# Cross-covariance attention: V moved up by one unit, and a tail written out by hand after the last gram

## The chip, the cores and the metric

The kernel runs on one core of a Trainium2 chip. The core has five engines with an instruction stream each: TensorE (PE; its weight loads are listed apart as PEld), VectorE (DVE), ScalarE (ACT), GpSimd (POOL) and SyncE (SP), which here issues every transfer between the chip's main memory (HBM) and the on-chip memory. The engines run side by side and wait for each other through semaphores; each works through its own instructions in the order in which the program wrote them. Matrix products land in PSUM, from where ACT or DVE copies them out. The metric is the device time of one execution in microseconds (us); the median of several runs is compared.

## The reference

Q, K and V have 8 batches, 12 heads, 512 positions and 64 features, all float32. Attention runs over the features, not over the positions:

```python
Q_norm = Q / (np.linalg.norm(Q, axis=-2, keepdims=True) + 1e-10)
K_norm = K / (np.linalg.norm(K, axis=-2, keepdims=True) + 1e-10)
attn = np.einsum('bhnd,bhne->bhde', Q_norm, K_norm)
attn = np.exp(attn - np.max(attn, axis=-1, keepdims=True))
attn = attn / (np.sum(attn, axis=-1, keepdims=True) + 1e-10)
return np.einsum('bhnd,bhde->bhne', V, attn)
```

So each head needs a 64x64 matrix of logits, which is complete only when all 512 positions of Q and K are in, a softmax over its rows, and then a product of V with that small matrix.

## The kernel before

The 96 heads are taken four at a time: a unit is four heads, and there are U = 24 units. For each unit Q, K and V are one transfer of 512 KB each, and so is the output. In all, SP issues 96 transfers.

What is done for a unit u, by the names of the functions:

- `load_qk`, `load_v`, `store`: the transfers, all on SP.
- `cast_q`, `cast_k` (DVE): Q and K to bf16, side by side in one tile `qkb`. `cast_v` (ACT): V to bf16, tile `vb`.
- `grams` (PE, 64 products): the product of [Q K] with itself, accumulated over the positions in the PSUM tile `gbuf`. One result holds the sums of squares on its diagonal and the raw logits off it. There is one `gbuf`, so the next unit's grams wait until this one's are read.
- `norms` (DVE, then POOL): the diagonal into `nsq` by four reductions, then its power -0.5 on POOL into `rq`. `keep_kq` (ACT): the logits, still unscaled, into `kq`.
- `scale_k` (DVE): `kq` times the norms of K gives `kqs`. `logits` (PE): transposes it into PSUM. `scale_q` (DVE): times the norms of Q gives `sl`. `exps` (ACT): the exponential `ex`.
- `normalise` (DVE, three instructions): row sums, their reciprocals, and the normalised bf16 matrix into the upper half of one of three buffers `ab`. `doubled` (PE, then ACT): a copy of it into the lower half, so that two heads can be multiplied at once. The logits and this duplicate share one PSUM tile.
- `vtrans` (PE, eight transposes, then an ACT copy): V with the features on the partitions, tile `vt`.
- `outs` (PE, 16 products; ACT, two copies): the output of the unit through two PSUM buffers `po` into `so`, which `store` sends.

The order is written by hand. One loop, over steps s, issues for several units at a time, each function at its own distance behind the grams of unit s:

```python
LOAD_AHEAD = 3
V_AHEAD = LOAD_AHEAD - 3
STORE_LAG = 6
```

Q and K are loaded three units ahead, V for the unit of the same step. Softmax work (`scale_k`, `logits`, `scale_q`, `exps`) is for unit s-1; `normalise`, `doubled`, `cast_v` and `vtrans` for unit s-2; `outs` for unit s-3; the store for unit s-6. A call outside 0 to U-1 is skipped by `on`, so the loop runs three steps past the last gram, to s = U+2, and its last three steps hold only what is left over. Because each engine keeps the program's order, a function's place in the step is also its place in its engine's queue.

Of the kernel before, what the change touches and what calls it, by code (L numbers as in the profile page):

```python
# [24 lines left out]
def kernel(  # L25
# [7 lines left out]
    nc = tc.nc  # L33
    B, H, N, _ = Q.shape
    assert N == NV * R and Q.shape[3] == D
    U = B * H // HU
# [17 lines left out]
    ps_o = ctx.enter_context(tc.tile_pool(name="ps_o", bufs=2, space=bass.MemoryType.PSUM))  # L54

    LOAD_AHEAD = 3
    V_AHEAD = LOAD_AHEAD - 3
    STORE_LAG = 6

    qf, kf, vf, vb, qkb, nsq, rq, kqs, sl, ex, vt, so, kq = ({} for _ in range(13))  # L60

    def load_qk(u):
        qf[u] = qp.tile([128, R, D], F32, name="qf")
        kf[u] = qp.tile([128, R, D], F32, name="kf")
        nc.sync.dma_start(out=qf[u].rearrange("p t d -> p (t d)"), in_=Qf[u])  # L65
        nc.sync.dma_start(out=kf[u].rearrange("p t d -> p (t d)"), in_=Kf[u])  # L66

    def load_v(u):
        vf[u] = vp.tile([128, SV, TP * 2 * D], F32, name="vf")
        nc.sync.dma_start(out=vf[u], in_=Vf[u])  # L70

    def store(u):
        nc.sync.dma_start(out=Of[u], in_=so[u].rearrange("p s t d -> p s (t d)"))
# [5 lines left out]
    def cast_k(u):  # L79
        nc.vector.tensor_copy(qkb[u][:, :, D:], kf[u])  # L80

    def cast_v(u):
        w = vb[u] = vbp.tile([128, SV, TP, 2 * D], BF16, name="vb")
        nc.scalar.copy(w.rearrange("p s t d -> p s (t d)"), vf[u])  # L84

    def grams(u):

# [22 lines left out]
    def scale_k(u):  # L110

        kk = kqs[u] = small.tile([128, HU, D], F32, name="kqs")
        nc.vector.tensor_tensor(  # L113
            out=kk[D:], in0=kq[u][D:], in1=rq[u][D:, :, None].to_broadcast([D, HU, D]), op=ALU.mult,
        )

    def logits(u):
        for h in range(HU):
            nc.tensor.transpose(lg[:, h, :], kqs[u][D:, h, :], ident[D:, D:])  # L119

    def scale_q(u):
        s = sl[u] = small.tile([D, HU, D], F32, name="sl")
        nc.vector.tensor_tensor(out=s, in0=lg, in1=rq[u][0:D, :, None].to_broadcast([D, HU, D]), op=ALU.mult)  # L123

    def exps(u):
        e = ex[u] = small.tile([D, HU, D], F32, name="ex")
        nc.scalar.activation(e, sl[u], AF.Exp)  # L127

    def normalise(u):
        s = small.tile([D, HU], F32, name="esum")  # L130
        nc.vector.reduce_sum(out=s, in_=ex[u], axis=AX.X)  # L131
        ri = small.tile([D, HU], F32, name="rinv")
        nc.vector.reciprocal(ri, s)
        a = abuf[u % len(abuf)]
        nc.vector.tensor_tensor(out=a[0:D, :, 0, :], in0=ex[u], in1=ri[:, :, None].to_broadcast([D, HU, D]), op=ALU.mult)  # L135

    def vtrans(u):

        ps = ps_v.tile([128, SV, TP, 128], BF16, name="vps")
        for g in range(SV):  # L140
            for t in range(TP):
                nc.tensor.transpose(ps[:, g, t, :], vb[u][:, g, t, :], identb)  # L142
        w = vt[u] = vtp.tile([128, SV, TP, 128], BF16, name="vt")
        nc.scalar.copy(w, ps)  # L144

    def doubled(u):

        a = abuf[u % len(abuf)]
        nc.tensor.matmul(dup[D:], identb[0:D, 0:D], a[0:D, :, 0, :], tile_position=(0, D))  # L149
        nc.scalar.copy(a[D:, :, 1, :], dup[D:])  # L150

    def outs(u):
        s = so[u] = sop.tile([128, SV, TP, 2 * D], F32, name="so")
        a = abuf[u % len(abuf)]
        for g in range(SV):
            po = ps_o.tile([128, TP, 2 * D], F32, name="po")
            for t in range(TP):
                for x in range(2):
                    rows = slice(MV * x, MV * (x + 1))
                    nc.tensor.matmul(  # L160
                        po[rows, t, :], vt[u][:, g, t, rows],
                        a[:, 2 * g + x].rearrange("p a d -> p (a d)"), tile_position=(0, MV * x),
                    )
            nc.scalar.copy(s[:, g], po)  # L164
# [6 lines left out]

    for u in range(LOAD_AHEAD):
        load_qk(u)

    ident = const.tile([128, 128], F32, name="ident")
    make_identity(nc, ident)
# [10 lines left out]
    def on(f, u):  # L187
        if 0 <= u < U:
            f(u)

    on(cast_q, 0)
    on(cast_k, 0)
    for s in range(U + 3):
        on(load_qk, s + LOAD_AHEAD)
        on(load_v, s + V_AHEAD)
        on(store, s - STORE_LAG)
        on(cast_v, s - 2)
        on(cast_q, s + 1)
        on(normalise, s - 2)
        on(scale_k, s - 1)  # L200
        on(grams, s)
        on(norms, s)
        on(cast_k, s + 1)
        on(doubled, s - 2)
        on(keep_kq, s)
        on(outs, s - 3)
        on(logits, s - 1)
        on(scale_q, s - 1)
        on(exps, s - 1)
        on(vtrans, s - 2)  # L210
    for u in range(U + 3 - STORE_LAG, U):
        store(u)


# [28 lines left out]
```

## Time and profile before

Four runs took 136.02 to 136.83 us, with a median of 136.13. The profile is of one more execution, which took 136.24 us; its span from the first to the last instruction is 134.5 us, with 1.74 us around it.

| engine | busy us | share of the span | instructions |
|---|---|---|---|
| PE (matmul) | 88.3 | 66% | 2232 |
| PEld (weight load) | 68.4 | 51% | 2232 |
| DVE | 94.6 | 70% | 360 |
| ACT | 97.9 | 73% | 169 |
| POOL | 36.1 | 27% | 35 |
| transfers of the kernel | - | 95.7% of 16 DMA engines | 96 |

No compute engine is busy for more than three quarters of the span. The transfers read 37.75 MB and write 12.58 MB, with a mean of 374 GB/s over the span.

How to read what follows: a row of the timeline has the start in us from the beginning of the span, the duration in us, the engine, the line of the kernel, the operation, what it writes <- what it reads, the number of merged instructions, and in brackets how long the engine had stood idle and for whom. SPq is SP issuing a transfer. The chain of waits starts from the last instruction and goes back, at each step, to what released it. The rows of slices cut the span into 40 equal pieces; each digit is a share in tenths, with 9 for 90% or more. The granted clock is the share of its full speed at which TensorE was allowed to run; its mean here is 0.827.

### The profile page before, as it was taken

To read this page: it belongs to the slowest core of one execution; us is meant where nothing else is said; L and a number is where in the kernel's file an instruction comes from. 1 tells how busy PE (TensorE), PEld (TensorE's weight loads), DVE (VectorE), ACT (ScalarE), POOL (GpSimd) and SP (SyncE) were. 2 spreads that over 40 slices of the span, in tenths; PEclk is the share of its full clock that TensorE was granted. 3 is DMA by queue.
4 is the path that set the end of the run, shared out by engine and by line. 5 is a ranking of instruction groups with operands and counts; after the bars stand their busy time and mean duration, and the time that the engine had idled before them with its cause. 6 is when DMAs were issued, how large, how long until landed. Compare 5 with 4: busy or idle time off the path is not lost.

```text
span 134.5 us, 5399 instructions
## 1 busy us (share of the span) xinstructions
PE 88.3 (66%) x2232; PEld 68.4 (51%) x2232; DVE 94.6 (70%) x360; ACT 97.9 (73%) x169; POOL 36.1 (27%) x35
## 2 busy tenths in 40 slices
PE   0146669766674986566645974979984669957630
PEld 0135457555453865454433862756862556745420
DVE  0477957988987898887956887967887967654100
ACT  3011268898889898988966796697796697999950
POOL 7023233244413541343123033033033032120000
PEclk9999999999999599999995599555589965586555
DMA  4999999999999999999999999999999999997444
GB/s 146 388 417 403 403 405 401 398 396 403 397 413 403 414 401 411 408 405 401 410 413 404 413 403 414 411 412 408 409 408 410 402 409 409 399 376 277 162 156 156
DMA packets 19991, 50.67 MB, mean 377 GB/s; under 512 B 1536, under 2 KB 1536, under 8 KB 19968
## 3 DMA queue, kind: packets, MB, share of 16 engines
q1 hardware_dynamic: 19968, 50.34, 95.7%
q8 instruction: 17, 0.28, 0.8%
q14 instruction: 6, 0.05, 0.1%
HBM read 37.75 MB, written 12.58 MB: 374 GB/s over the span
## 4 chain that ended last, share of the span: by engine, by line
DMA 47%; ACT 17%; PE 14%; DVE 9%; issue 6%; SPq 3%; ACTq 0%; DVEq 0%
DMA vf<-in_V_dram 47%; PE gram L91 5%; ACT so L164 4%; ACT vb L84 4%; ACT vt L144 3%; DVE scr L103 3%; PE vps L142 3%; PE lgdup L119 3%; PE po L160 3%; ACT ab L150 2%; ACT ex L127 2%; ACT kq L96 1%; SPq L65 1%; SPq L66 1%; DVE kqs L113 1%
## 5 line engine op out<-in xcount | busy, mean ns | idle before, releaser
L108 POOL TENSOR_TENSOR rq<-nsq,mhalf 128x4 f32<-128x4 f32 x24 | 33.7, 1402 | 82.7 <-DVE nsq L103 82.7
L91 PE MATMUL gram<-qkb 32*128 32x128 bf16 x1536 | 35.0, 254 | 13.1 <-DVE qkb L80 8.9
L91 PEld LDWEIGHTS <-qkb 32*128 32x128 bf16 x1536 | 29.2, 113 | 17.2 <-DVE qkb L80 9.4
L84 ACT CAST vb<-vf 128x1024 bf16<-128x1024 f32 x24 | 25.1, 1047 | 13.0 <-DMA vf<-in_V_dram 13.0
L164 ACT COPY so<-po 128x512 f32<-128x512 f32 x48 | 25.8, 589 | 1.5 <-PE po L160 1.0
L160 PEld LDWEIGHTS <-vt 128*64 128x64 bf16 x384 | 15.3, 136 | 19.5 <-ACT vt L144 14.1
L103 DVE CUSTOM_DVE_ANT_0 scr<-gram,ident 128x128 f32<-128x128 f32 x96 | 22.2, 287 | 3.6 <-PE gram L91 3.1
L144 ACT COPY vt<-vps 128x1024 bf16<-128x1024 bf16 x24 | 24.0, 1001 | 0.6
L160 PE MATMUL po<-ab,vt 128*64 128x128 bf16 x384 | 20.1, 263 | 2.3 <-ACT vt L144 1.2
L77 DVE CAST qkb<-qf 128x1024 bf16<-128x1024 f32 x24 | 16.4, 682 | 7.0 <-DMA qf<-in_Q_dram 6.9
L119 PE MATMUL lgdup<-ident,kqs 64*64 64x64 f32 x96 | 12.1, 260 | 12.7 <-ACT ab L150 12.7
L123 DVE TENSOR_TENSOR sl<-lgdup,rq 64x256 f32<-64x256 f32 x24 | 9.9, 414 | 13.0 <-PE lgdup L119 12.3
L142 PE MATMUL vps<-identb,vb 128*128 128x128 bf16 x192 | 18.8, 254 | 0.1
L96 ACT COPY kq<-gram 64x256 f32<-64x256 f32 x24 | 8.8, 367 | 13.5 <-DVE nsq L103 13.3
L80 DVE CAST qkb<-kf 128x1024 bf16<-128x1024 f32 x24 | 16.5, 689 | 0.5 <-DMA kf<-in_K_dram 0.5
L149 PE MATMUL lgdup<-ab,identb 64*64 64x256 bf16 x24 | 7.9, 330 | 13.1 <-DVE ab L135 12.9
L119 PEld LDWEIGHTS lgdup<-ident,kqs 64*64 64x64 f32 x96 | 7.5, 128 | 17.0 <-ACT ab L150 16.1
L142 PEld LDWEIGHTS <-vb 128*128 128x128 bf16 x192 | 13.7, 114 | 3.2 <-issue 1.7
L131 DVE TENSOR_REDUCE esum<-ex 64x4 f32<-64x256 f32 x24 | 9.8, 408 | 3.8 <-ACT ex L127 3.7
L127 ACT ACTIVATE ex<-sl 64x256 f32<-64x256 f32 x24 | 10.0, 417 | 1.7 <-DVE sl L123 1.5
L113 DVE TENSOR_TENSOR kqs<-kq,rq 64x256 f32<-64x256 f32 x24 | 10.1, 422 | 0.8
L135 DVE TENSOR_TENSOR ab<-ex,rinv 64x256 bf16<-64x256 f32 x24 | 10.0, 416 | 0.8
(14 smaller groups left out, 27.5 us busy)
## 6 DMA issues: line engine op xcount, KB each, us to landing
qf<-in_Q_dram SPq DMA_DIRECT2D x24, 512.0 KB, 10.1
kf<-in_K_dram SPq DMA_DIRECT2D x24, 512.0 KB, 10.1
vf<-in_V_dram SPq DMA_DIRECT2D x24, 512.0 KB, 10.1
out_dram<-so SPq DMA_DIRECT2D x24, 512.0 KB, 10.1
```

What stands on the lines that cost most here:

```text
L77: nc.vector.tensor_copy(qkb[u][:, :, 0:D], qf[u])
L80: nc.vector.tensor_copy(qkb[u][:, :, D:], kf[u])
L84: nc.scalar.copy(w.rearrange("p s t d -> p s (t d)"), vf[u])
L91: nc.tensor.matmul(gbuf[:, h, 0:2 * D], x, x, start=(t == 0), stop=(t == R - 1), tile_position=(NV * h, 0))
L103: nc.vector.tensor_tensor_reduce(out=scr, in0=gbuf[:, h, 0:2 * D], in1=ident, scale=1.0, scalar=1e-20, op0=ALU.mult, op1=ALU.add, accum_ou ...
L108: nc.gpsimd.tensor_tensor(out=r, in0=n2, in1=mhalf, op=ALU.pow)
L119: nc.tensor.transpose(lg[:, h, :], kqs[u][D:, h, :], ident[D:, D:])
L127: nc.scalar.activation(e, sl[u], AF.Exp)
L142: nc.tensor.transpose(ps[:, g, t, :], vb[u][:, g, t, :], identb)
L144: nc.scalar.copy(w, ps)
L160: nc.tensor.matmul(po[rows, t, :], vt[u][:, g, t, rows], a[:, 2 * g + x].rearrange("p a d -> p (a d)"), tile_position=(0, MV * x),)
L164: nc.scalar.copy(s[:, g], po)
```

## The change

There are three things in it. V is loaded, cast and transposed one unit closer to the grams: `load_v` for unit s+1 in step s, with the V of unit 0 loaded ahead of the loop between Q, K of unit 2 and Q, K of unit 3; `cast_v` and `vtrans` for unit s-1. Within a step, `scale_k` now stands ahead of `normalise`. And the loop ends with the last grams, at s = U-1; what is left over then, including the outputs of the last three units, is written out call by call, with the last unit's V cast on DVE instead of ACT.

```diff
-    V_AHEAD = LOAD_AHEAD - 3
+    V_AHEAD = LOAD_AHEAD - 2
...
-    def cast_v(u):
+    def cast_v(u, copy=nc.scalar.copy):
         w = vb[u] = vbp.tile([128, SV, TP, 2 * D], BF16, name="vb")
-        nc.scalar.copy(w.rearrange("p s t d -> p s (t d)"), vf[u])
+        copy(w.rearrange("p s t d -> p s (t d)"), vf[u])
...
     for u in range(LOAD_AHEAD):
         load_qk(u)
+        if u - 2 >= 0:
+            load_v(u - 2)
...
-    for s in range(U + 3):
+    for s in range(U):
         on(load_qk, s + LOAD_AHEAD)
         on(load_v, s + V_AHEAD)
         on(store, s - STORE_LAG)
-        on(cast_v, s - 2)
+        on(cast_v, s - 1)
         on(cast_q, s + 1)
+        on(scale_k, s - 1)
         on(normalise, s - 2)
-        on(scale_k, s - 1)
         on(grams, s)
...
-        on(vtrans, s - 2)
-    for u in range(U + 3 - STORE_LAG, U):
+        on(vtrans, s - 1)
+
+    last = U - 1
+    scale_k(last)
+    logits(last)
+    scale_q(last)
+    exps(last)
+    normalise(last - 1)
+    doubled(last - 1)
+    outs(last - 2)
+    cast_v(last, nc.vector.tensor_copy)
+    normalise(last)
+    doubled(last)
+    vtrans(last)
+    outs(last - 1)
+    outs(last)
+    for u in range(U - STORE_LAG, U):
         store(u)
```

## The prediction

> **What bounds the kernel now.** I read the page's slices first, then the chain of waits, then SP's timeline, then the last 20 us of all engines. The slices (40 of 3.36 us; DMA busy in tenths, granted TensorE clock in tenths) say that transfers fill the span except for its last four slices:
>
> ```profile
> PEclk9999999999999599999995599555589965586555
> DMA  4999999999999999999999999999999999997444
> ```
>
> So there are two parts to ask about: a stream paced by transfers, and a tail of about 13 us in which they no longer bound. The chain of waits (start, us, what) shows where one passes into the other:
>
> ```profile
> 102.18 10.07 DMA vf<-in_V_dram
> ...
> 112.33 1.05 ACT vb L84
> ...
> 124.92 1.06 ACT vb L84
> 126.00 0.37 ACT ab L150
> 126.36 0.02 issue
> 126.39 1.08 ACT so L164 x2
> 127.47 0.04 issue
> 127.50 1.02 ACT vt L144
> 128.53 0.04 issue
> 128.57 0.66 PE po L160 x8
> 129.23 0.02 issue
> 129.25 0.58 ACT so L164
> ```
>
> The last landing that anything waits for is that of V of unit 20 (casts stand at 107.26, 112.33, 116.42, 120.83, 124.92; the last is unit 23's, so the second is unit 20's). After it the chain is ACT work almost without a gap, with short passes through PE. The last eviction ends at 129.25 + 1.07 = 130.32 (two copies from 129.25); its store is issued at 130.35, moves data from about 131.25 to 132.75 and lands 2.8 us after issue; the span ends at 134.5, so 4.2 us lie behind the last eviction. They stay.
>
> SP's timeline, every issue of which waits for an earlier landing, gives the price of a place in the stream:
>
> ```profile
> 100.89 0.34 SPq L66 DMA_DIRECT2D kf<-in_K_dram  x1
> 102.18 0.38 SPq L70 DMA_DIRECT2D vf<-in_V_dram  x1
> 103.49 0.39 SPq L73 DMA_DIRECT2D out_dram<-so  x1
> 104.68 0.37 SPq L70 DMA_DIRECT2D vf<-in_V_dram  x1
> ```
>
> 1.19 to 1.31 us each, eight in flight (10.1 us to landing): one place is 1.27 us.
>
> **Part 1: V one step earlier (V_AHEAD, the prologue's load_v, cast_v and vtrans at s-1).** It removes no byte. A step still issues q, k, v, store, and cast_v still takes the V issued two steps before, but that V belongs to a later unit: from the prologue on, one more V stands ahead of each step. Counting the queue: before, step 22 opens with V of unit 20, transfer 48+21+14 = 83rd (48 of q and k, 21 V, 14 stores). After, it opens with V of unit 21, 84th: SP passes q, k, V, store in the same cycle, with load_v(0) as 7th transfer instead of 9th and load_qk(3) pushed from 7th to 8th. ACT idled 0.88 us for V before the cast at 112.33, and 1.05 at most steps since 82 us, so this place is on the path: **+1.27 us** on everything from there, last grams included. At the start it is the same: cast_v(0) now stands before the copy of step 1's grams and takes 1.05 us there, about 0.75 late for that copy (12.65 to 13.4), but step 2 waits for the 10th transfer (landed about 17.8, when the 18th is issued) instead of the 9th (16.47) anyway, the same 1.3. Between 24 and 57 us the chain is engine work at 4.3 us a step against 5.07 for four transfers, so whatever the start loses is caught up to the stream's pace; the stream's place is not.
>
> **Part 2: scale_k ahead of normalise (DVE, loop).** Nothing is added; normalise comes 0.44 us later (start to start of the 0.42 us kqs). In the step at 104 us ab would end at 106.85, not 106.41, so the duplicate on PE starts 0.44 later than 106.46; its copy on ACT starts only at 108.33, behind the V cast that waited for DMA. Cover is left, cost nothing; without cover 0.44 a step. In steps at half clock the duplicate waits for grams till 112.11 and ab at 111.94 is still in time. Where the step waits for exp, kqs fits into DVE's 0.5 us gap.
>
> **Part 3: the hand-ordered tail.** The rows it is summed from (start, duration; the same instructions in the old tail):
>
> ```profile
> 118.16 0.08 DVE L103 DVE_READ_ACCUMULATOR2_ANT nsq<- 128x1 f32 x1
> 118.38 1.01 POOL L108 TENSOR_TENSOR rq<-nsq,mhalf 128x4 f32<-128x4 f32 x1 [3.75 <-DVE nsq L103]
> 118.52 0.45 PE L119 MATMUL lgdup<-ident,kqs 64*64 64x64 f32 x4
> 119.08 0.41 DVE L123 TENSOR_TENSOR sl<-lgdup,rq 64x256 f32<-64x256 f32 x1 [0.85 <-PE lgdup L119]
> ...
> 126.38 1.04 PE L142 MATMUL vps<-identb,vb 128*128 128x128 bf16 x8
> ```
>
> First the ACT work behind the last kq copy (ends 118.64): before, 2.5 us of step 23, then two casts of V, three vt copies among the rest; after, V casts of units 22 and 23 and vt of unit 21 are gone from it (22 and vt 21 have run earlier, 23 goes to DVE): 1.05 + 1.05 + 1.00 = 3.1 us less. How much of that survives the new waits I worked forward on the clock of before, with PE full until 122 us and half from there (as granted then):
> rq to 119.39; DVE free of sl(22) at 119.50, kqs(23) to 119.94; logits to 120.44; sl(23) 120.55 to 120.97; exp(23) behind vt(22), to 121.44. DVE: normalise(22) = 0.45+0.20+0.42 from 121.00, to 122.07. PE: duplicate(22) at 122.12, outs(21) 122.42 to 123.48. ACT: ab(22) 122.63, so(21) 123.03 to 124.1; it idled 1.1 us before ab(22). DVE: V cast 122.10 to 122.79, normalise(23) to 123.87. PE: duplicate(23) 123.92, V transposes 124.22 to 125.26, outs(22) to 126.32. ACT: ab(23) 124.35, vt(23) 125.34 to 126.33, so(22) 126.23 to 127.30. outs(23) waits for vt(23), then for the two po buffers freed at 126.81 and 127.29; so(23) ends at **128.57**, 1.75 us before 130.32. What is late next is thus vt(23): behind normalise(23), not behind ACT's backlog.
>
> The V cast on DVE is not in the trace; the nearest row is the cast of K, 0.69 us (1024 f32 to bf16, strided output); ACT's 1.05 is the other end. I take 0.69; at 1.05 normalise(23) is 0.36 later, on the path. V of unit 23 becomes the 88th transfer; the 82nd has landed when the 90th is issued, at 111.03, so the 88th lands near 111.03 + 6 x 1.27 = 118.6, while DVE reaches it at 122.10 + 1.27: no wait. rq took 1.01 with DVE idle and 1.32 in most steps; DVE is idle there again, so 1.01; else 0.2 to 0.3 more. The waits for the shared logits/duplicate tile fall within the sums: each reader is done before the next writer. Stores: units 22 and 23 are now evicted 1.3 us apart instead of 2.9, and one store moves data for 1.4 us: up to 0.1 us.
>
> **The clock, rule against row.** The windows from 109 to 118 show PE busy 85 to 100% of the time at a granted clock of 0.50 to 0.59, likewise 1.00 busy at 0.50 from 90 to 93. The Trainium skill ("TensorE: Matmul & The Clock Gate", Part 1) says the clock goes full after about 3.4 us of sustained activity. By the rule my denser tail runs full: so(23) ends 127.78, gain 2.54; by the row, half throughout, 128.75, gain 1.57. The row decides; the mixture above is nearest to the old tail.
>
> **Sum.** -1.75 + 1.27 = -0.48, with the stores' overlap about -0.4; a full clock in steps 22 and 23 (half before: grams 1.89 against 1.07) could give up to 0.5 more. I take -0.5. The profiled execution took 136.24 with span 134.5; its span would be 134.0 and its time 135.7. The median is 136.13, 0.11 lower: **135.6 us**. Its own range: 134.8 (full clock, -1.3) to 136.3 (half clock, slow rq, DVE cast at 1.05).
>
> **Rivals.**
> R1, the place in the stream costs nothing: completions have slack or the clock makes it good, and the tail's 1.75 stands: **134.4**. For: after 119 us the DMA share falls to 0.87, engines do not finish together. Against: ACT waits for V in nearly every step from 70 to 112.
> R2, slower: a hole in the landings. SP's issues jump from 13.66 to 16.53 and from 65.20 to 68.14, 1.6 us over the usual step each time. The first is the landing of the first V, which now comes before step 1. If the new order sets one more such hole ahead of the last grams, it moves everything behind: 135.6 + 1.6 = **137.2**; it decides from 1.2 us on. Against: neither hole lies in the last 45 us, and bytes and queue are the same.
> R3, an exchange of equals: half clock throughout, rq 1.32 and overlapping stores leave 1.57 - 0.2 - 0.1 = 1.27 to pay for the place: **136.1**. For: the clock from 123 on; against: it takes every cost at its worse end.
>
> **Chances.** What a measurement can tell here from no change is about 0.5%, 0.68 us. Forecast 0.52 (faster 0.27, same 0.24, slower 0.01, as it lies near the edge); R1 0.13, faster; R2 0.18 (slower 0.17, same 0.01); R3 0.17 (same 0.11, faster 0.03, slower 0.03). Sums: faster 0.43, same 0.36, slower 0.21. The range 134.2 to 137.1 leaves out R2's upper half and the edge of R1.
>
> **What would show it.** Step 22's V cast at about 113.6 (part 1; at 112.3 R1 holds; beyond 115, R2). Last grams ending near 118.5. The exp of unit 23 about 3 us behind the last norm. ACT idle about a microsecond ahead of ab(22), then vt(23) close behind the transposes. A last eviction at 129.8. I am wrong if ACT waits elsewhere in the tail, or if loop steps cease to take 5.07 us.

## The result, and the profile after

The changed kernel takes **135.38 us** (median of 36 runs, 134.13 to 136.35), against 136.17 for the kernel before in the same comparisons (55 runs, 135.58 to 137.27). The ratio is 0.9935, with a 95% interval of 0.9919 to 0.9950: about 0.9 us faster (0.7 to 1.1 by the interval). The forecast was 135.6, a gain of 0.5. The profiled execution took 135.85 us with a span of 134.1, so it is one of the later ones; its positions are used below for the mechanism and the medians for the times. Its mean granted clock, 0.707, is the lowest of the 36 (0.768 to 0.854 in the others), but the times hardly follow that clock: at 0.768 one execution took 134.91 us and another 135.97.

The slices of the changed kernel, to be held against those of before:

```profile
PEclk9999999877777667766765765557657655557555
DMA  4999999999999999999999999999999999998354
```

Transfers still fill the span up to the last four slices. The clock digits stay at 5 to 8 from the eighth slice to the end: in this execution TensorE wasn't granted its full clock in the later loop either, and not in the denser tail.

ACT's timeline behind the last V that anything waits for (start, us, engine, line, operation, what it writes <- what it reads, count, and in brackets the idle time before it and for whom):

```profile
113.98 1.05 ACT L84 CAST vb<-vf 128x1024 bf16<-128x1024 f32 x1 [0.87 <-DMA vf<-in_V_dram]
...
119.92 0.37 ACT L96 COPY kq<-gram 64x256 f32<-64x256 f32 x1 [0.21 <-DVE nsq L103]
...
122.55 0.42 ACT L127 ACTIVATE ex<-sl 64x256 f32<-64x256 f32 x1
123.91 0.37 ACT L150 CAST ab<-lgdup 64x256 bf16<-64x256 f32 x1 [0.94 <-PE lgdup L149]
124.42 1.07 ACT L164 COPY so<-po 128x512 f32<-128x512 f32 x2
125.59 0.37 ACT L150 CAST ab<-lgdup 64x256 bf16<-64x256 f32 x1
126.56 1.01 ACT L144 COPY vt<-vps 128x1024 bf16<-128x1024 bf16 x1 [0.60 <-PE vps L142]
127.47 1.08 ACT L164 COPY so<-po 128x512 f32<-128x512 f32 x2
128.79 1.07 ACT L164 COPY so<-po 128x512 f32<-128x512 f32 x2 [0.24 <-PE po L160]
```

Two things are to be read from it. The first row is step 22's V cast: it stood at 112.33 before, so all that follows starts 1.65 us later. And from that row to the end of the last eviction it is 129.86 - 113.98 = 15.88 us, where it was 130.32 - 112.33 = 17.99. The change pays at the front and gets 2.11 us back behind it. Nearly all of this lies behind the last norm of unit 23, which ends at 119.88 here and ended at 118.24 before:

```profile
119.80 0.08 DVE L103 DVE_READ_ACCUMULATOR2_ANT nsq<- 128x1 f32 x1
```

From there to the end of the last eviction it is 9.98 us, where it was 12.08. The chain of waits (start, us, what) now runs through DVE, where before it ran through ACT:

```profile
121.14 0.43 DVE kqs L113
...
122.10 0.42 DVE sl L123
122.52 0.34 DVE esum L131
...
123.08 0.42 DVE ab L135
123.50 0.60 DVE vb L84
124.10 0.34 DVE esum L131
...
124.67 0.43 DVE ab L135
...
125.14 0.42 PE lgdup L149
125.55 0.98 PE vps L142 x8
```

### The profile page after: what moved, and what is told of

It reads as the page before. It is cut to its first block, busy times and chain, and to the rows that moved or that the text cites. A ratio compares the mean times of both kernels' runs of the same rounds, so it can differ in the third digit from the quotient of the medians.

```text
span 134.1 us, 5393 instructions
## 1 busy us (share of the span) xinstructions
PE 94.2 (70%) x2232; PEld 73.2 (55%) x2232; DVE 95.4 (71%) x361; ACT 96.6 (72%) x168; POOL 35.5 (26%) x35
## 4 chain that ended last, share of the span: by engine, by line
DMA 63%; DVE 9%; PE 8%; ACT 8%; issue 3%; SPq 3%; POOL 2%; POOLq 0%; DVEq 0%; ACTq 0%
DMA vf<-in_V_dram 63%; ACT so L164 3%; PE gram L91 3%; DVE scr L103 2%; ACT vb L84 2%; POOL rq L108 2%; PE vps L142 2%; DVE ab L135 2%; PE lgdup L119 2%; SPq L66 1%; DVE esum L131 1%; SPq L65 1%; DVE kqs L113 1%; PE po L160 1%; ACT ab L150 1%
## 5 line engine op out<-in xcount | busy, mean ns | idle before, releaser
L108 POOL TENSOR_TENSOR rq<-nsq,mhalf 128x4 f32<-128x4 f32 x24 | 33.1, 1377 | 84.9 <-DVE nsq L103 84.9
L91 PE MATMUL gram<-qkb 32*128 32x128 bf16 x1536 | 39.1, 274 | 10.1 <-DVE qkb L80 7.8
L91 PEld LDWEIGHTS <-qkb 32*128 32x128 bf16 x1536 | 32.8, 122 | 14.5 <-DVE qkb L80 8.1
L84 ACT CAST vb<-vf 128x1024 bf16<-128x1024 f32 x23 | 24.1, 1046 | 18.0 <-DMA vf<-in_V_dram 18.0
L160 PEld LDWEIGHTS <-vt 128*64 128x64 bf16 x384 | 15.9, 137 | 15.7 <-issue 14.9
L142 PE MATMUL vps<-identb,vb 128*128 128x128 bf16 x192 | 20.2, 269 | 1.6 <-ACT vb L84 1.6
L160 PE MATMUL po<-ab,vt 128*64 128x128 bf16 x384 | 20.6, 269 | 0.6 <-ACT so L164 0.6
L142 PEld LDWEIGHTS <-vb 128*128 128x128 bf16 x192 | 14.7, 119 | 4.9 <-ACT vb L84 1.9
L150 ACT CAST ab<-lgdup 64x256 bf16<-64x256 f32 x24 | 8.8, 367 | 3.2 <-PE lgdup L149 2.6
L113 DVE TENSOR_TENSOR kqs<-kq,rq 64x256 f32<-64x256 f32 x24 | 10.1, 422 | 1.1
## 6 DMA issues: line engine op xcount, KB each, us to landing
qf<-in_Q_dram SPq DMA_DIRECT2D x24, 512.0 KB, 10.1
kf<-in_K_dram SPq DMA_DIRECT2D x24, 512.0 KB, 10.1
vf<-in_V_dram SPq DMA_DIRECT2D x24, 512.0 KB, 10.1
out_dram<-so SPq DMA_DIRECT2D x24, 512.0 KB, 10.1
```

The costliest lines, as they stand in the source:

```text
L91: nc.tensor.matmul(gbuf[:, h, 0:2 * D], x, x, start=(t == 0), stop=(t == R - 1), tile_position=(NV * h, 0))
L108: nc.gpsimd.tensor_tensor(out=r, in0=n2, in1=mhalf, op=ALU.pow)
L160: nc.tensor.matmul(po[rows, t, :], vt[u][:, g, t, rows], a[:, 2 * g + x].rearrange("p a d -> p (a d)"), tile_position=(0, MV * x),)
```

## The experiments

My theory was: the change is one place in the transfer stream (a loss) plus a shorter tail (a larger gain). Rival A: the place costs nothing, and only the amount of ACT work in the tail counts. Rival B: only the written-out order gains. All times are ratios to the kernel before, measured beside it. "Tail" is the time from step 22's V cast to the end of the last eviction in the profiled execution. The last column counts from the end of the last norm instead: the stretch between the two differs between executions, and so does the clock granted in it (5.90 us in the change, with a clock of 0.50; 5.62 in the V part alone, with 1.00 up to 116 us), so the last column is the better one to compare tails by.

| kernel | ratio, 95% interval | V cast of step 22, us | tail, us | behind the last norm, us |
|---|---|---|---|---|
| before | 1 | 112.33 | 17.99 | 12.08 |
| the change | 0.9935, 0.9919 to 0.9950 | 113.98 | 15.88 | 9.98 |
| V part alone | 0.9983, 0.9963 to 1.0002 | 113.66 | 15.83 | 10.21 |
| written-out tail alone | 0.9906, 0.9882 to 0.9930 | 112.89 | 16.99 | 11.10 |
| change, stores one step later | 0.9891, 0.9860 to 0.9922 | 113.35 | 15.88 | 9.98 |
| change, last V cast on ACT | 1.0001, 0.9974 to 1.0028 | 113.76 | 16.57 | 10.99 |
| change, normalise first | 0.9923, 0.9898 to 0.9947 | 114.23 | 15.72 | 10.09 |
| before, stores one step later | 0.9911, 0.9878 to 0.9943 | not readable | | |
| change, V one more step ahead | 0.9951, 0.9925 to 0.9977 | 113.90, no wait | 16.09 | 9.87 |
| change, last V cast and transposes first | 0.9858, 0.9823 to 0.9892 | 113.73 | 15.45 | 9.55 |
| the same, cast in the empty place | 0.9839, 0.9797 to 0.9880 | 113.95 | 14.64 | 8.74 |
| change, stores three steps later | 0.9791, 0.9750 to 0.9832 | 109.75 | 15.05 | 10.01 |
| tail alone, stores three steps later | 0.9779, 0.9740 to 0.9818 | 108.39 | 16.99 | 11.10 |
| cast in the empty place, stores three steps later | 0.9802, 0.9759 to 0.9845 | 109.96 | 14.86 | 9.13 |

**The two halves.** First the V part alone, with the loop of before:

```diff
-    V_AHEAD = LOAD_AHEAD - 3
+    V_AHEAD = LOAD_AHEAD - 2
...
         load_qk(u)
+        if u - 2 >= 0:
+            load_v(u - 2)
...
-        on(cast_v, s - 2)
+        on(cast_v, s - 1)
...
-        on(vtrans, s - 2)
+        on(vtrans, s - 1)
```

> The change's V part alone (V loaded, cast and transposed one unit closer to the grams); the loop keeps its three extra steps and normalise stays ahead of scale_k. My theory (the change is a place in the transfer stream that costs 1.3 to 1.6 us, plus ACT work taken out of the tail): the V cast of step 22 stands at 113.6 to 114.0 us as in the changed kernel, not at 112.3; behind the last kq copy 2.05 us of ACT work (one V cast, one vt copy) is gone, so the last eviction ends near 129.5 and the time is 0.5 to 0.9 us below before. Rival A (the place costs nothing): V cast of step 22 near 112.4, time about 2 us below before. Rival B (the written-out tail is what gains, the V part only costs): 1.3 us above before.

The V cast stands at 113.66, and the last eviction ends at 129.49, as the theory said; rival A's 112.4 and rival B's loss of 1.3 us are both out. But the time is only 0.2 us below before (interval 0.5 below to no change), less than the 0.5 to 0.9 expected. The profiled execution (135.45 us) is faster than this kernel's own median (135.88). Part of it may be the clock, which was full from 110 to 116 us in this execution; its slices, to be held against those of the change:

```profile
PEclk9999999999999689965579975579869869868555
```

From the V cast to the last norm it is 0.28 us shorter than the change (5.62 against 5.90). What else makes most executions slower than this one wasn't found, and stays open. Behind the last norm the V part alone needs 10.21 us, 0.23 more than the whole change: in the traces most of the tail's gain, 1.87 of 2.10 us, comes with V's move, in the old loop. In the times the change is 0.65 us below the V part alone.

Then the tail alone, with V in its old place:

```diff
-    for s in range(U + 3):
+    for s in range(U):
...
+    last = U - 1
+    scale_k(last)
+    logits(last)
+    scale_q(last)
+    exps(last)
+    cast_v(last - 1)
+    normalise(last - 1)
+    doubled(last - 1)
+    vtrans(last - 1)
+    outs(last - 2)
+    cast_v(last, nc.vector.tensor_copy)
+    normalise(last)
+    doubled(last)
+    vtrans(last)
+    outs(last - 1)
+    outs(last)
```

> The written-out tail alone: V stays two units behind the grams and in its old place in the stream; the tail therefore also holds the V cast of unit 22 on ACT and its transposes. My theory: V cast of step 22 at 112.3, no place is paid, and the tail shortens by about 1.1 us though ACT has 2.05 us more to do in it than in the changed kernel (part of it falls into the idle time ahead of the duplicate of unit 22): last eviction near 129.2, 1.1 us below before, so at least as fast as the whole change. Rival A (the place costs nothing, ACT work is all that counts): about 1 us slower than the whole change, near before.

It is 1.3 us below before, and its tail is 1.0 us shorter. Rival A expected about no gain. The profiled execution (136.10 us) is the slowest of this kernel's 22, so its positions are late (the V cast was expected at 112.3, and the last eviction, at 129.88, near 129.2); its lengths are what counts. So the written-out tail alone brings at least what the whole change brings; whether it brings more (0.9906 against 0.9935) can't be said for certain, since the intervals overlap a little. ACT's timeline of this kernel shows how its extra work was absorbed: the cast of V of unit 22 sits in what is idle time in the changed kernel.

```profile
121.86 0.42 ACT L127 ACTIVATE ex<-sl 64x256 f32<-64x256 f32 x1
122.18 1.03 ACT L84 CAST vb<-vf 128x1024 bf16<-128x1024 f32 x1
123.32 0.37 ACT L150 CAST ab<-lgdup 64x256 bf16<-64x256 f32 x1
124.40 1.01 ACT L144 COPY vt<-vps 128x1024 bf16<-128x1024 bf16 x1 [0.71 <-PE vps L142]
```

**The price of a place.** A store issued later leaves one transfer fewer ahead of the loads, and nothing else changes. It was tried in the changed kernel and in the one before:

```diff
-    STORE_LAG = 6
+    STORE_LAG = 7
```

> The changed kernel with each store issued one step later, so one store fewer stands ahead of every step's loads; nothing else differs. My theory: one place in the stream is bought back, the V cast of step 22 moves from 113.98 to about 112.7 and the whole tail with it: 1.3 us below the changed kernel, 2.0 us below before. Rival A (a place costs nothing): no change against the changed kernel.

> The kernel before with each store issued one step later. My theory (one place in the stream ahead of the last grams costs 1.3 us in either kernel): V cast of step 22 at about 111.0, 1.3 us below before. Rival A (a place costs nothing): no change against before.

Before gains 1.2 us, as expected. The changed kernel gains only about 0.6 (0.9891 against 0.9935; 0.1 to 1.1 by the two intervals), half of what was expected. In its profiled execution the V cast moved only to 113.35, after a wait of 2.00 us. The transfer of that V was issued at 102.27, 1.56 us earlier than in the change, so the place was bought back; but it took 11.1 us to land instead of 10.1. SP's issues in that execution jump once late in the stream, where other steps take 1.3:

```profile
107.33 0.44 SPq L70 DMA_DIRECT2D vf<-in_V_dram  x1
109.51 1.65 SPq L73 DMA_DIRECT2D out_dram<-so  x2
```

Such jumps come in every execution, most of them at other places in each, so one position is uncertain by some 0.3 to 0.7 us. Why the medians gain only half stays open. The position in the profile of before with late stores can't be read: that execution took 316.9 us, with TensorE busy for 299.6 us of it, and is left out of the ratio.

Three stores instead of one gave a clearer answer:

```diff
-    STORE_LAG = 6
+    STORE_LAG = 9
```

> The changed kernel with each store issued three steps later, so three stores fewer stand ahead of every step's loads. My theory (each place in the stream ahead of the last grams costs 1.27 us, one for one): V cast of step 22 at about 110.2 instead of 113.98, time 3.8 us below the changed kernel, somewhat less if the steps meet the engines' own pace (4.3 us) on the way: 2.5 to 3.8 below, 131.6 to 132.9. Rival (a place is worth half, as the first experiment with one store suggested with 0.6): 1.5 to 2 us below the changed kernel. Rival A (a place costs nothing): no change.

The V cast is at 109.75, against 113.98 in the change, so the three places are worth 4.2 us here, one for one or a little more. By the positions the half price is refuted; the time alone would have fitted it, as the next lines explain. The last eviction ends at 124.80, 5.06 us earlier than in the change. But the time is only 2.0 us below the change, less than the 2.5 to 3.8 expected: now 6.5 us, not 4.2, lie between the last eviction and the end of the span. The windows of that kernel (window in us, busy time and number of instructions of PE, PEld, DVE, ACT and POOL, granted clock, DMA share, GB/s) show what took over; the last eviction ends ahead of them:

```profile
125.00:125.50 0.50, 0.00 (x0) 0.00 (x0) 0.00 (x0) 0.00 (x0) 0.00 (x0) 0.50 1.07 410
126.50:127.00 0.50, 0.00 (x0) 0.00 (x0) 0.00 (x0) 0.00 (x0) 0.00 (x0) 0.50 1.05 406
127.50:128.00 0.50, 0.00 (x0) 0.00 (x0) 0.00 (x0) 0.00 (x0) 0.00 (x0) 0.50 0.58 225
128.50:129.00 0.50, 0.00 (x0) 0.00 (x0) 0.00 (x0) 0.00 (x0) 0.00 (x0) 0.50 0.06 25
129.00:129.50 0.50, 0.00 (x0) 0.00 (x0) 0.00 (x0) 0.00 (x0) 0.00 (x0) 0.50 0.06 25
129.50:130.00 0.50, 0.00 (x0) 0.00 (x0) 0.00 (x0) 0.00 (x0) 0.00 (x0) 0.50 0.02 8
```

The DMA engines run full until 127 and then finish one after another; a share of 0.06 is one engine of 16, which still works for 1.2 us when the others are done. The end is bound by transfers now, which is why this kernel's gain stops halfway.

The tail alone with the same late stores asked whether moving V pays once the stream is relieved:

> The written-out tail alone (V two units behind the grams, in its old place) with each store issued three steps later. My theory (moving V costs its place and, with the written-out tail in hand, brings less than that): 0.3 to 0.7 us below the changed kernel with the same stores. Rival (with the stores out of the way the place no longer counts and the 2.05 us less ACT work does): 0.5 to 1 us above it.

133.16 us against 133.31, the same within the intervals. Neither expectation can be seen in the time, since both kernels end with the transfers. Its V cast, at 108.39, is 1.36 us ahead of the other's: the place itself is still there.

**The tail's parts.** The last V cast on ACT:

```diff
-    cast_v(last, nc.vector.tensor_copy)
+    cast_v(last)
```

> The changed kernel with the last unit's V cast on ACT, at the same place of the program. My theory (in the tail vt of unit 23 waits for its transposes): the cast stands behind so of unit 21, from about 125.4 to 126.45, the transposes and vt of unit 23 move back by about 1.0 us: 1.0 us above the changed kernel, near before. Rival (DVE's queue bounds the tail, ACT has idle time to hide the cast): 0.3 us below the changed kernel, as normalise of unit 23 starts 0.7 us earlier.

It takes back the whole gain of the change (1.0001), 0.9 us, as the theory said. Behind the last norm it is 1.01 us longer than the change:

```profile
124.84 1.06 ACT L84 CAST vb<-vf 128x1024 bf16<-128x1024 f32 x1
127.03 1.01 ACT L144 COPY vt<-vps 128x1024 bf16<-128x1024 bf16 x1 [0.74 <-PE vps L142]
```

The rival's idle time exists (1.01 us ahead of the duplicate of unit 22), but ACT keeps its order, so the cast, which stands behind it, can't use it. This also tells order and cast apart: with V moved, the written-out order with that cast on ACT is no better than the old loop (1.0001 against 0.9983; 10.99 against 10.21 us behind the last norm). With V in its old place the two were not run apart. The swap of scale_k and normalise, undone:

```diff
-        on(scale_k, s - 1)
         on(normalise, s - 2)
+        on(scale_k, s - 1)
```

> The changed kernel with normalise ahead of scale_k again in the loop. My theory (the swap is hidden): same as the changed kernel within 0.3 us. Rival (the swap is what shortens the loop's engine-bound steps or the last ones): 0.4 us or more above the changed kernel.

No difference (0.9923 against 0.9935, well inside the intervals): neither a gain nor a cost of the swap can be seen, and the rival's 0.4 us is out. Then the chain of waits was put to the test, by taking the V cast and the transposes of the last unit out of it:

```diff
     last = U - 1
+    cast_v(last, nc.vector.tensor_copy)
     scale_k(last)
...
     exps(last)
+    vtrans(last)
...
-    cast_v(last, nc.vector.tensor_copy)
     normalise(last)
     doubled(last)
-    vtrans(last)
```

> The changed kernel with the last unit's V cast put first in the tail (DVE stands idle there for 0.8 us) and its transposes and vt copy behind the exp of unit 23 (PE and ACT stand idle there). My theory (the tail's chain is scale_q, normalise 22, V cast, normalise 23, duplicate, transposes, vt, so): cast and transposes leave the chain; last eviction near 128.2 instead of 129.86, 1.3 to 1.7 us below the changed kernel. Rival (ACT's work is the bound of the tail, order is worth little): within 0.4 us of the changed kernel.

About 1.0 us below the change (0.5 to 1.6 by the two intervals), less than expected but over the rival's 0.4. In the trace the gain is smaller: behind the last norm 0.43 us are gone, and the last eviction ends at 129.18, not near 128.2. DVE's order shows what took the rest: the cast could not use the idle time ahead of scale_q of unit 22, since it stands behind it, and pushed scale_k back to 121.71 (121.14 in the change).

```profile
120.66 0.42 DVE L123 TENSOR_TENSOR sl<-lgdup,rq 64x256 f32<-64x256 f32 x1 [1.03 <-ACT so L164]
121.00 0.68 DVE L84 CAST vb<-vf 128x1024 bf16<-128x1024 f32 x1
...
121.71 0.42 DVE L113 TENSOR_TENSOR kqs<-kq,rq 64x256 f32<-64x256 f32 x1
```

In the next kernel the cast takes the place that the last step leaves empty:

```diff
         on(cast_k, s + 1)
+        if s == U - 1:
+            cast_v(s, nc.vector.tensor_copy)
...
     last = U - 1
-    cast_v(last, nc.vector.tensor_copy)
     scale_k(last)
```

> As the kernel with the last V cast and its transposes first in the tail, but with that cast in the place that the cast of K leaves empty in step 23, directly behind the last norms and ahead of scale_q of unit 22, so that scale_k of unit 23 is not pushed back by 0.6 us. My theory (the chain starts with that scale_k): 0.5 us below the kernel it comes from, 1.6 us below the changed kernel. Rival (V of unit 23 lands only just ahead, near 119.0, and the chain does not start there): no difference from the kernel it comes from.

The cast starts at 119.77 without a wait and scale_k stands at 121.35; the tail is 0.81 us shorter than its parent's, by either column. In the time the step is 0.3 us and inside the intervals, so there it isn't shown. Against the change it is 1.3 us; the expected 1.6 was not quite reached. Both improvements together:

> Both together: stores three steps later, last V cast in the empty place of step 23, its transposes behind the exp of unit 23. If the stream's places and the tail's chain add up: 1.3 to 1.7 us below the changed kernel with late stores, about 130.5 to 131.5. If the stores that are left then bound the end (nine of them at 1.27 us behind the last load): within 0.5 us of the changed kernel with late stores.

133.45 us, no better than late stores alone: the second case. The last eviction ends at 124.82, and the span 6.6 us later: transfers set the end.

**V yet one step ahead.** One more V in the prologue and one more in front of every step:

```diff
-    V_AHEAD = LOAD_AHEAD - 2
+    V_AHEAD = LOAD_AHEAD - 1
...
-        if u - 2 >= 0:
-            load_v(u - 2)
+        if u - 1 >= 0:
+            load_v(u - 1)
```

> The changed kernel with V loaded yet one more step ahead, still cast one unit behind the grams. My theory in its simple form (every V put ahead costs a place): 1.3 us above the changed kernel. In its finer form (the place is only paid because ACT's cast at the head of a step waits for the transfer that lands last; with V early the wait passes to K of the next unit, which is needed two thirds of a step later): ACT no longer waits for V, and the time is 0.5 to 1.5 us below the changed kernel.

Both forms of the theory missed: the time is the change's within the intervals (0.9951 against 0.9935). ACT does not wait for V any more, but the wait didn't pass to K late in the step. It passed to Q, whose cast heads DVE's queue, and everything of the step stands behind it:

```profile
108.11 0.69 DVE L77 CAST qkb<-qf 128x1024 bf16<-128x1024 f32 x1 [1.04 <-DMA qf<-in_Q_dram]
...
108.83 0.42 DVE L113 TENSOR_TENSOR kqs<-kq,rq 64x256 f32<-64x256 f32 x1
```

## Why the prediction was right, point by point

**The bound.** Transfers pace the stream, an engine chain the last 15 to 18 us. The price of a place moved the V casts as the theory said, except with stores one step later (half of it) and with V yet one step ahead, where another wait took over.

**Part 1, the place.** Priced at 1.27. In the two profiled executions it was 1.65, but these contain the scatter of the stream. Counting issues takes it out. Before, the cast waited for the 83rd transfer, issued at 102.18; in the change it waits for the 84th, and the 83rd and 84th are issued at

```profile
102.53 0.34 SPq L66 DMA_DIRECT2D kf<-in_K_dram  x1
103.83 0.38 SPq L70 DMA_DIRECT2D vf<-in_V_dram  x1
```

So 0.35 is scatter and 1.30 the place. Over all profiled kernels with six steps of store lag and a waiting V cast, the cast of step 22 stands at 112.33 and 112.89 where V is in its old place (mean 112.61), and at 113.98, 113.66, 113.76, 114.23, 113.73 and 113.95 where it is one unit ahead (mean 113.89): a difference of 1.28, uncertain by some 0.3, since the old place has two executions only. R1, the free place, is refuted by that and by the gain of 1.2 us when the kernel before issues its stores one step later.

**Part 2, the swap.** Costed at nothing; undoing it changed nothing that can be seen.

**Part 3, the tail.** Forecast as 1.75 us shorter, measured as 2.11. The order of events was the predicted one: ACT idle ahead of ab(22) for 0.94 us (1.1), vt(23) behind its transposes at 126.56 (126.61 with the place added), the last eviction ending at 129.86 (129.84). That the last figure fits so closely is luck: the place came out 0.38 larger and the tail 0.36 shorter than forecast. The mis-sized term is DVE's spacing. I stepped from sl to esum and from ab to the V cast with 0.45 us each, and 0.70 from the cast to esum; these came out at 0.34, 0.34 and 0.61:

```profile
122.10 0.42 DVE L123 TENSOR_TENSOR sl<-lgdup,rq 64x256 f32<-64x256 f32 x1 [0.54 <-PE lgdup L119]
122.44 0.40 DVE L131 TENSOR_REDUCE esum<-ex 64x4 f32<-64x256 f32 x1
...
123.08 0.42 DVE L135 TENSOR_TENSOR ab<-ex,rinv 64x256 bf16<-64x256 f32 x1
123.42 0.68 DVE L84 CAST vb<-vf 128x1024 bf16<-128x1024 f32 x1
...
124.03 0.40 DVE L131 TENSOR_REDUCE esum<-ex 64x4 f32<-64x256 f32 x1
```

Together that is 0.31 of the 0.36. The V cast on DVE took 0.68, as the row of K's cast said; on ACT it would have taken the whole gain back.

**The sum.** The tail's 2.11 less a place of 1.28 to 1.30 is 0.8 us, which is what the times show (0.8 by the medians, 0.9 by the ratio). The forecast of 0.48 had the sign, the waits and the place right, and the tail 0.36 too small.

**The clock.** Row against rule, the row was right. The granted clock was 0.50 from 109 to 120 us, 0.75 from 120.5 to 123.5, and 0.50 from 124 to the end; it was not full anywhere in the tail, and the transposes of the last unit took 1.03 us, as at half clock (0.62 at full clock before):

```profile
125.49 1.03 PE L142 MATMUL vps<-identb,vb 128*128 128x128 bf16 x8
```

The clock fell about where the mixture had it, at 122 us plus the place, but from 0.75 and not from full.

**The rivals.** R2's holes exist, but they stayed where they were: SP's 17th and 56th issues come late before (16.53 and 68.14) and in the change (16.17 and 67.70). With eight transfers in flight the 17th waits for the ninth landing, which was the first V before and is K of unit 3 now, so that hole did not belong to the first V. No kernel here shows that the new order adds one ahead of the last grams. R3's exchange of equals fails because the tail gained more than its worse ends.

**What I did not see.** I added up the two halves of the change as if each were needed. Behind the last norm V's move alone saves 1.87 us, the written-out tail alone 0.98, and both together 2.10. ACT's idle time ahead of ab(22), which the forecast names, can take part of the V work that part 1 removes: the tail alone is only 1.1 us longer than the change's for 2.05 us more work. What is left is about the price of the place, so the written-out tail alone, with its V cast on DVE, does as well.

## What to carry to other kernels

When transfers run in one queue that is always full, a buffer loaded earlier is a place taken from everything behind it, and it is paid for where that queue's landings set the pace (the first V put ahead cost 1.3 us, a second one nothing that shows in the time); look for something that can give the place back, such as stores that nobody waits for. Issuing them three steps later moved the last eviction forward by 5 us here, and the best of these kernels run at 133.2 to 133.5 us, 2% below before. In a tail written by hand, follow each engine's queue: work taken from a busy engine only counts where that engine isn't waiting at the time, and an instruction can use another's idle time only if it stands ahead of what waits.

## What the runs showed of the hardware

- The 16 DMA engines do not finish together. At the end of the kernel with late stores, a share of 0.06, one engine, remains for 1.2 us, and the span ends 1.7 us after that.
- The landings scatter: in the profiled executions SP's issues, 1.3 us apart, jump by 0.3 to 1.7 us more at three to eight places. Three of these come in all 13 readable executions: the 11th issue, the 17th (once the 18th) and the 56th or 57th, whatever is loaded there; the others differ. Positions near the end differ by up to 0.6 us between kernels with the same order of transfers.
- POOL's power on 128x4 values took 1.01 us while DVE stood idle and 1.32 us when DVE's V cast ran at the same time (the kernel with the cast in the empty place). There scale_k of unit 23 starts at 121.35, just behind it.
- The granted clock of the change's profile is 0.75 from 26 to 44 us, between the 0.50 and 1.00 of most other stretches. Eight transposes of V take 0.71 us there, 0.62 at 1.00 and 1.03 at 0.50.
- One execution of the kernel before with late stores took 316.9 us, with TensorE busy for 299.6; the others of it took 134.3 to 136.2. The same eight transposes took 2.61 us in it, though its granted clock is recorded as 1.00. The cause is open.
